# A higher priority for the split of the mixers' weights into high and low parts

## The chip, the cores and the metric

The kernel runs on one core of one Trainium2 chip. The metric is the device time in microseconds (us), the median over runs. Engines: PE is TensorE (matmuls; PEld its weight loads), DVE is VectorE, ACT is ScalarE, POOL is GpSimd, SP is SyncE, which here only issues DMAs.

## What is computed

Two layers of a network over 512 tokens of width 1024, all in float32. Each layer is a mixer followed by a mixture of experts, with norms, shifts, scales and gates (`mod`) that come from a small condition vector:

```python
for layer in range(DEPTH):                       # DEPTH = 2
    mod = cond @ w_ada[layer] + b_ada[layer]
    sh1, sc1, gt1, sh2, sc2, gt2 = jnp.split(mod[:, None, :], 6, axis=-1)
    u = rms_norm(h, norm1[layer]) * (1.0 + sc1) + sh1
    m = mixer_ab(u, ...) if layer % 2 == 0 else mixer_c(u, ...)
    h = h + gt1 * m
    u = rms_norm(h, norm2[layer]) * (1.0 + sc2) + sh2
    h = h + gt2 * hier_moe(u, ...)               # 32 experts, top 2 of one group
return rms_norm(h, final_norm)
```

Both mixers begin with a projection `u @ w_in` and end with one `y @ w_out`; between them, `mixer_ab` has a gated linear recurrence and a gated linear attention (4 heads), `mixer_c` a gated delta rule (8 heads, chunks, triangular solves).

## The kernel before

**Stages.** Layer 0's mixer runs from the start to about 295 us of the span, its router and experts to about 800 us; layer 1's mixer from 802 to about 1165 us, its router and experts to the end. The experts' stage goes through 16 pairs of experts, whose weights stream from HBM.

**The mixers' matmuls in three parts.** The mixers' matmuls take inputs of a rounded type (`F32R`). To keep float32 accuracy every factor is the sum of a high part, rounded, and a low part, the rest. `mm3` (L432) makes three matmuls of each pair: high by high (L435), high by low (L436), low by high (L437). For a weight block of 128 x 512, `split` (L424) makes the parts: ACT copies the raw block into `whi`, which rounds it (L428), and POOL subtracts `whi` from the raw block into `wlo` (L429). Both come from the pool `whl`, which has three buffers of each name. There are 136 such blocks. The input `u` gets its two parts in `u_block` (L552): ACT (L557), DVE (L558), and for the low part DVE or POOL by turns (L559).

**Steps.** A step is the work on one split block: `step_T` (L439) and `steps_rows` (L470) give pairs of functions, `prep`, which calls `split` (and, for output weights, first multiplies them by the gate, L480, on DVE and POOL by turns), and `mm`, a generator of the step's 12 matmuls. `run_steps` (L497) writes, ahead of step i, the `prep` of the steps up to i + 2; between the halves of a step it ticks the `Stream`, a small clock in which the other work of the mixers (gates, attention, keys, queries, solves, recurrences, modulation vectors) waits as generators with lags in ticks. Raw weight blocks are loaded by SP (L136) into a ring of two tiles; `raw_done` asks for the load of the next one when the last `split` that reads a tile has been written.

**What sets the order on an engine.** The program is written in one sequence, but the framework orders each engine's instructions anew: it plays the program through in a model of time, and at each point gives an engine, of those instructions whose inputs and buffers are there in the model, the one that ranks first. The rank is the place in the program. `tc.high_priority(PRI)` with `PRI = 80` ranks what is written inside it as if it stood 80 instructions earlier; before the change it is used for the first one-hot matrices of each layer's experts, for the gates' logits of `mixer_c` and for two exponentials of the router. `keep_in_program_order` ties an instruction behind the one written before it on its engine. On the chip each engine then runs its list strictly in that order, and waits at an instruction whose inputs or buffer are not there yet.

**Layer boundary.** At the end of layer 0 a loop over overflowing experts (`overflow`, L1718 to L1720; its count is read at run time) stands between the layers; all engines pass it together. Behind it `restart` (L1947) makes the row norms: ACT takes a square root (L419), DVE its reciprocal (L420), ACT and DVE scale a row block each (L1954, L1955), and PE turns the blocks (L564) before `u_block` makes `u`. `startup` (L1874) does the like in layer 0, with modulation vectors that it must compute first.

**Names that the prediction uses.** `yAhi`, `yAlo` (L673, L674): high and low parts of the linear recurrence's result, wanted by the first output steps. L755 `ex`: exponentials of the attention's decays; L792 `qs`: its scaled queries. In `mixer_c`: L1017 to L1020 the convolution and `Silu` of keys, queries and values (`kT`, `qT`, `vT`); L1035 the turning of the keys on PE; L1088 keys by queries; L1138 `X`, part of the triangular solve, and L1146 the matmuls that read it; L912 `orow`, the normed output rows, and L916 their turning.

Of the kernel before, what the change touches and what calls it, by code (L numbers as in the profile page):

```python
# [7 lines left out]
F32 = mybir.dt.float32  # L8
# [3 lines left out]
AF = mybir.ActivationFunctionType  # L12
# [16 lines left out]
PRI = 80  # L29
# [62 lines left out]
class Build:  # L92
# [331 lines left out]
    def split(self, src, shape):  # L424
        nc = self.nc
        hi = self.whl.tile(shape, F32R, name="whi", tag="whi")
        lo = self.whl.tile(shape, F32R, name="wlo", tag="wlo")
        nc.scalar.activation(hi, src, AF.Copy)  # L428
        nc.gpsimd.tensor_sub(lo, src, hi.bitcast(F32))  # L429
        return hi, lo  # L430

    def mm3(self, p, lhs, rhs, start, stop):  # L432
# [1563 lines left out]
```

## Time and profile before

| | |
|---|---|
| runs before | 1705.33, 1702.36, 1694.67 us; median 1702.36 |
| profiled execution | 1700.37 us; span 1698.2 us |
| mean granted clock of PE | 0.983 |
| busy: PE, DVE, ACT, POOL | 1623.4, 766.6, 522.6, 398.7 us |
| read from HBM | 492.21 MB, 291 GB/s over the span |

The span is the time between the first and the last event of the profiled execution; its own time, taken outside, is 2.2 us longer. A row of groups reads: line, engine, operation, output <- inputs, partitions x elements, count | busy us, mean ns of one | idle us of the engine just before them, with what ended that idle time. A row of waits reads: engine, what it was to make, line <- what it waited for: total us, times, longest. A row of the timeline reads: start us, duration us, engine, line, operation, count, and in brackets the idle time before it and what ended it. A row of windows reads: stretch, length, then busy us and count for PE, PEld, DVE, ACT and POOL, then PE's granted clock (1.00 is full), the DMA engines' mean busy share, and GB/s. SPq is the queue of SP.

### The profile page before, as it was taken

Reading aid. Unit: us, or ns where it says so; the run is one execution under the profiler, and the core shown is the slowest. Engines: PE = TensorE matmul, PEld = TensorE weight load, DVE = VectorE, ACT = ScalarE, POOL = GpSimd, SP = SyncE. Lnnn points to the kernel's source line nnn. Section 1 sums busy time; section 2 is a strip of 40 time slices with the busy share of each in tenths; the row PEclk is TensorE's granted clock in tenths of the full one; section 3 lists DMA queues with packets and bytes.
Section 4 is the critical chain, followed back from the end, with each engine's and each line's share of the span. In section 5 each row is a group of like instructions: output and inputs, shape, how many; then the busy total and the mean of one; then the engine's idle time right before and its main releaser. Section 6 shows DMA issues by size and latency. Waiting matters only on the chain. (4 is left out here: it accounts for less than half of the span.)

```text
span 1698.2 us, 23027 instructions
## 1 busy us (share of the span) xinstructions
PE 1623.4 (96%) x8890; PEld 973.7 (57%) x8890; DVE 766.6 (45%) x1770; ACT 522.6 (31%) x1034; POOL 398.7 (23%) x346
## 2 busy tenths in 40 slices
PE   6999999899999999998999999999899999999996
PEld 3665667454554555454666777787454555455453
DVE  2344553433333233234687787764324233233324
ACT  4665323210110111013646667555110111011013
POOL 2464542210100101001544353553100101001011
PEclk9999999999999999999899999999999999999998
DMA  8765646689999999995244333266699999999992
GB/s 306 230 216 172 247 162 227 264 350 386 414 411 413 413 411 414 411 411 158 75 154 146 125 103 122 75 224 233 231 374 412 412 411 414 411 412 413 412 406 99
DMA packets 156561, 496.02 MB, mean 292 GB/s; under 512 B 16472, under 2 KB 43668, under 8 KB 141088
## 3 DMA queue, kind: packets, MB, share of 16 engines
q1 hardware_dynamic: 155488, 493.23, 75.5%
q8 instruction: 72, 1.18, 0.3%
q10 hardware_dynamic: 960, 1.28, 0.2%
q14 instruction: 41, 0.34, 0.1%
HBM read 492.21 MB, written 2.10 MB: 291 GB/s over the span
## 5 line engine op out<-in xcount | busy, mean ns | idle before, releaser
L1538 PE MATMUL ps<-w,XTm 128*64 128x512 f32 x2048 | 447.1, 593 | 0.0
L1538 PEld LDWEIGHTS ps<-w,XTm 128*64 128x64 f32 x2048 | 161.7, 137 | 267.5 <-issue 260.2
L429 POOL TENSOR_TENSOR wlo<-w,whi 128x512 fp32r<-128x512 f32 x136 | 185.9, 1374 | 233.7 <-ACT whi L428 230.9
L1592 PE MATMUL ps<-w,hT 128*64 128x512 f32 (+1 forms) x1056 | 229.2, 584 | 1.0 <-ACT hT L1570 1.0
L1561 DVE TENSOR_TENSOR gg<-gg,ps 128x512 f32<-128x512 f32 x32 | 22.0, 687 | 377.8 <-PE ps L1538 377.7
L435 PE MATMUL ps<-w,whi 128*128 128x512 f32 x384 | 163.1, 425 | 0.4 <-ACT w L557 0.4
L436 PE MATMUL ps<-w,whi 128*128 128x512 f32 x384 | 154.1, 402 | 2.0 <-POOL w L559 1.5
L437 PE MATMUL ps<-w,wlo 128*128 128x512 f32 x384 | 153.7, 401 | 2.1 <-POOL wlo L429 2.1
L1592 PEld LDWEIGHTS ps<-w,hT 128*64 128x64 f32 x1056 | 81.8, 136 | 129.0 <-issue 116.0
L1615 DVE TENSOR_TENSOR w<-w,ps 128x512 f32<-128x512 f32 (+1 forms) x248 | 149.2, 662 | 6.9 <-PE ps L1606 5.5
L1547 POOL CAST sel<-ident 32x128 fp32r<-32x128 f32 x32 | 9.0, 280 | 590.4 <-PE ps L1575 532.7
L1596 POOL TENSOR_TENSOR yl<-y,yh 128x512 fp32r<-128x512 f32 x60 | 76.5, 1275 | 250.8 <-ACT yh L1595 250.8
L1595 ACT ACTIVATE yh<-y 128x512 fp32r<-128x512 f32 (+1 forms) x66 | 40.8, 618 | 294.5 <-DVE y L1594 293.6
L428 ACT ACTIVATE whi<-w 128x512 fp32r<-128x512 f32 x136 | 84.7, 627 | 143.9 <-PE ps L436 79.2
L1462 PE MATMUL ps<-Dm,hhi 128*128 128x256 f32 x512 | 125.8, 288 | 0.0
L1462 PE MATMUL ps<-Dm,hlo 128*128 128x256 f32 x512 | 123.3, 283 | 0.0
L1594 DVE SCALAR_TENSOR_TENSOR y<-ps,wsl,gate 128x512 f32<-128x512 f32 (+1 forms) x66 | 48.4, 734 | 150.5 <-issue 76.0
L1462 PEld LDWEIGHTS ps<-Dm,hhi 128*128 128x128 f32 x512 | 101.3, 198 | 13.5 <-issue 12.7
L1570 ACT ACTIVATE hT<-ps 128x512 f32<-128x512 f32 x32 | 19.1, 598 | 284.5 <-PE ps L1568 266.2
L1606 PE MATMUL ps<-yh,dt 128*128 128x512 f32 (+1 forms) x264 | 105.9, 406 | 0.0
L1462 PEld LDWEIGHTS ps<-Dm,hlo 128*128 128x128 f32 x512 | 101.3, 198 | 0.1
L1606 PE MATMUL ps<-yl,dt 128*128 128x512 f32 (+1 forms) x264 | 100.9, 387 | 0.0
(522 smaller groups left out, 2345.5 us busy)
## 6 DMA issues: line engine op xcount, KB each, us to landing
w<-in_moe_w_dram SPq DMA_DIRECT2D x380, 1024.0 KB
w<-in_w_ada_dram SPq DMA_DIRECT2D x40, 1024.0 KB
w<-in_w_in_c_dram SPq DMA_DIRECT2D x16, 1024.0 KB
w<-in_w_in_ab_dram SPq DMA_DIRECT2D x10, 1024.0 KB
wst<-in_w_ada_dram SPq DMA_DIRECT2D x8, 1024.0 KB
w<-in_w_out_ab_dram SPq DMA_DIRECT2D x4, 1024.0 KB
w<-in_moe_w_dram SPq DMA_DIRECT2D x8, 512.0 KB
w<-in_w_out_c_dram SPq DMA_DIRECT2D x4, 1024.0 KB
```

Of the source, the lines that this page charges most:

```text
L428: nc.scalar.activation(hi, src, AF.Copy)
L429: nc.gpsimd.tensor_sub(lo, src, hi.bitcast(F32))
L435: mm(p, lhs[0], rhs[0], start=start, stop=False)
L436: mm(p, lhs[0], rhs[1], start=False, stop=False)
L437: mm(p, lhs[1], rhs[0], start=False, stop=stop)
L1462: nc.tensor.matmul(p, spread(src[:, t], k // 4)[k % 4], Dm[:, t].rearrange("p e s -> p (e s)"), start=t + i == 0, stop=t == NT - 1 and i == 1)
L1538: self.nc.tensor.matmul(ps[j][half[e]], X[:, k, half[e]], w, start=k == 0, stop=k == KD - 1)
L1592: nc.tensor.matmul(py[half[e]], hT[:, k, half[e]], w, start=k == 0, stop=k == 3)
L1594: nc.vector.scalar_tensor_tensor(y32, py, wsl, gate[:, c], op0=OP.mult, op1=OP.mult)
L1596: (nc.vector if last else nc.gpsimd).tensor_sub(yl[:, c], y32, yh[:, c].bitcast(F32))
L1606: mm = nc.tensor.matmul(p, dt[:, t * P:(t + 1) * P], y[:, s], start=i == 0, stop=i == 1)
L1615: nc.vector.tensor_add(h, h, p)
```

## The change

The two instructions of `split` are written inside `tc.high_priority(PRI)`. Nothing else changes: the same instructions, tiles, buffers and loads.

```diff
@@ -425,8 +425,9 @@ def split(self, src, shape):
         hi = self.whl.tile(shape, F32R, name="whi", tag="whi")
         lo = self.whl.tile(shape, F32R, name="wlo", tag="wlo")
-        nc.scalar.activation(hi, src, AF.Copy)
-        nc.gpsimd.tensor_sub(lo, src, hi.bitcast(F32))
+        with self.tc.high_priority(PRI):
+            nc.scalar.activation(hi, src, AF.Copy)
+            nc.gpsimd.tensor_sub(lo, src, hi.bitcast(F32))
         return hi, lo
```

## The prediction

> **What bounds the kernel now.** I read the page first, then the busy time by stage, then what TensorE (PE) waited for in the two mixer stages, then the timeline at each such wait.
>
> ```profile
> span 1698.2 us, 23027 instructions
> PE 1623.4 (96%) x8890; PEld 973.7 (57%) x8890; DVE 766.6 (45%) x1770; ACT 522.6 (31%) x1034; POOL 398.7 (23%) x346
> ...
> L429 POOL TENSOR_TENSOR wlo<-w,whi 128x512 fp32r<-128x512 f32 x136 | 185.9, 1374 | 233.7 <-ACT whi L428 230.9
> ...
> L428 ACT ACTIVATE whi<-w 128x512 fp32r<-128x512 f32 x136 | 84.7, 627 | 143.9 <-PE ps L436 79.2
> ```
>
> PE is busy 96% of the span; nothing else is over 45%. The change touches two lines: 136 roundings `whi` on ScalarE (627 ns each) and 136 subtractions `wlo` on GpSimd (1374 ns each). GpSimd waits for `whi` before `wlo`, and `whi` waits for PE, which must give a buffer back.
>
> ```profile
> 802.00:1165.00 363.00, 344.20 (x2261) 261.98 (x2261) 265.59 (x773) 220.67 (x463) 167.58 (x144) 0.97 0.39 129
> 28.00:295.00 267.00, 257.02 (x1336) 175.46 (x1335) 123.10 (x231) 125.20 (x253) 121.14 (x84) 0.98 0.60 207
> ```
>
> ```profile
> 1320.00:1640.00 320.00, 320.00 (x1634) 168.40 (x1634) 103.27 (x191) 37.69 (x64) 28.31 (x30) 1.00 1.02 412
> ```
>
> The columns are the stretch, its length, the busy time of PE, PEld, DVE, ACT and POOL, PE's granted clock, the DMA share and GB/s. The splits lie in the first two stretches (mixer of layer 1, mixer of layer 0). There PE is idle 363.00 − 344.20 = 18.8 us and 267.00 − 257.02 = 10.0 us, and the clock below 1.00 costs another 0.03 × 363 = 10.9 and 0.02 × 267 = 5.3 us. All that the mixers can give is thus about 45 us, 2.6% of the time, whatever its cause. The expert stage (third row) has no idle PE time, so what a mixer gains or loses reaches the end nearly whole.
>
> **What PE waited for.** Of this idle time only a little is a split that came late:
>
> ```profile
> PE ps L437 <- POOL wlo L429: 2.1, 2, 1.7
> ...
> PE ps L436 <- POOL w L559: 1.5, 2, 1.2
> ...
> PE ps L436 <- POOL wlo L429: 1.0, 2, 0.7
> ```
>
> ```profile
> PE ps L916 <- ACT orow L912: 3.1, 3, 1.9
> PE ps L1035 <- ACT kT L1020: 2.6, 1, 2.6
> PE ps L1088 <- ACT qT L1020: 2.0, 2, 1.4
> ...
> PE ps L1146 <- ACT X L1138: 1.4, 1, 1.4
> ```
>
> The first list is layer 0 from 28 to 340 us, the second layer 1 from 800 to 1190 us (total us, times, longest). In layer 0 `wlo` holds PE up 2.1 + 1.0 = 3.1 us in four waits. In layer 1 no wait of PE over 0.4 us ends with a split; PE waits there for other ScalarE work, that of the delta-rule chains.
>
> **The change, part by part.** No instruction is added or removed, no size changed. Each `whi` and `wlo` is ranked as if written 80 instructions earlier. The ordering happens before the run, in the framework's own model of time: an engine takes, of what is ready there, what is ranked first. A rounding for step i+2 is written just ahead of step i and is ready when step i−1 has returned its buffer (three buffers). So it already stands ahead of all that step i calls up; what the 80 add is that it passes work of the few steps before: convolutions, gates, decays, and GpSimd's other multiplications. On ScalarE everything passed by one `whi` comes 0.63 us later, on GpSimd everything passed by one `wlo` comes 1.37 us later.
>
> *Gain 1: the late splits of layer 0.* These are the three waits of PE that can be found in the timeline, with what stood ahead:
>
> ```profile
> 118.48 0.50 PE L436 MATMUL ps<-wlo,w 128*128 128x512 f32 x1 [0.72 <-POOL wlo L429]
> 149.34 0.50 PE L437 MATMUL ps<-w,wlo 128*128 128x512 f32 x1 [0.43 <-POOL wlo L429]
> 158.41 0.51 PE L437 MATMUL ps<-w,wlo 128*128 128x512 f32 x1 [1.68 <-POOL wlo L429]
> ```
>
> ```profile
> 113.41 3.78 POOL L674 TENSOR_TENSOR yAlo<-xc,yAhi 128x512 fp32r<-128x512 f32 x3
> 117.14 3.77 POOL L429 TENSOR_TENSOR wlo<-w,whi 128x512 fp32r<-128x512 f32 x3
> ...
> 153.81 4.55 POOL L429 TENSOR_TENSOR wlo<-w,whi 128x512 fp32r<-128x512 f32 x1 [2.36 <-ACT whi L428]
> ```
>
> ```profile
> 152.09 0.63 ACT L755 ACTIVATE l<-l 128x512 f32<-128x512 f32 x1 [1.49 <-DVE l L765]
> 152.63 0.58 ACT L792 ACTIVATE qs<-ps 128x512 f32<-128x512 f32 x1
> 153.11 0.62 ACT L428 ACTIVATE whi<-w 128x512 fp32r<-128x512 f32 x1
> ```
>
> At 117.14 `wlo` stands behind three `yAlo` subtractions (3.78 us) that nobody needs before the output steps; passing them removes the 0.72 us. At 153.11 `whi` comes after a decay exponential and a copy, with 1.49 us of idle ScalarE just before; passing both brings it 1.2 us forward, and up to 2.7 us if it takes the idle slot, against 1.68 us wanted. I take the three waits whole: −0.72 − 0.43 − 1.68 = **−2.8 us**, bounds −2.8 and 0 (if in the model the split is not ready earlier). The 4.55 us `wlo` is not a matter of order: it takes 4.55 instead of the mean 1.37 us because it runs beside VectorE's decay work, and it will meet such work wherever it is put. By the Trainium skill ("SBUF — State Buffer", section on the two separate sides) VectorE and GpSimd share one port pair under an exclusive lock, so the later of two such instructions stands still until the first ends. By that rule the third wait would only shrink if `wlo` also started ahead of the VectorE instruction; without it the gain would be about −1.2 us instead of −2.8.
>
> *The start.* `whi` of step 2 is written after the first modulated blocks `u` (L557–L559) and is now ranked ahead of blocks 1 to 3.
>
> ```profile
> 28.73 2.98 POOL L429 TENSOR_TENSOR wlo<-w,whi 128x512 fp32r<-128x512 f32 x2 [26.66 <-ACT whi L428]
> 31.66 1.28 POOL L559 TENSOR_TENSOR w<-uf,w 128x512 fp32r<-128x512 f32 x1
> 32.90 1.74 POOL L429 TENSOR_TENSOR wlo<-w,whi 128x512 fp32r<-128x512 f32 x1
> 34.60 1.26 POOL L559 TENSOR_TENSOR w<-uf,w 128x512 fp32r<-128x512 f32 x1
> ```
>
> ```profile
> 35.92 0.50 PE L436 MATMUL ps<-w,whi 128*128 128x512 f32 x1 [1.24 <-POOL w L559]
> ```
>
> GpSimd's order becomes `wlo` three times, then `u` block 1, then block 3. Block 1 moves from 31.66 to about 28.73 + 2.98 + 1.37 = 33.1 and ends at 34.4; block 3 ends at about 35.6 instead of 35.86. PE waits longer for block 1 but is held by block 3 either way. Net −0.3 to +0.3 us; I take 0.
>
> *Cost 1: the layer boundary.* Behind the overflow loop of layer 0, ScalarE starts layer 1 with the row norms; PE stands still until the first normalised rows:
>
> ```profile
> 802.25 1.28 ACT L419 ACT_TABLE_LOAD   x1 [1.22 <-DVEq L1720]
> ...
> 804.11 1.93 ACT L1954 ACTIVATE hn<-w,hr 128x512 f32<-128x512 f32 x3
> ...
> 806.14 0.62 ACT L428 ACTIVATE whi<-w 128x512 fp32r<-128x512 f32 x1
> 806.66 0.71 ACT L1954 ACTIVATE hn<-w,hr 128x512 f32<-128x512 f32 x1
> 807.27 1.13 ACT L428 ACTIVATE whi<-w 128x512 fp32r<-128x512 f32 x2
> ```
>
> ```profile
> 804.87 3.87 PE L564 MATMUL ps<-ident,hn 128*128 128x128 f32 x16 [7.25 <-ACT hn L1954]
> ```
>
> Counting the code, some 55 instructions lie between the first norm and the first `whi`, fewer than 80, so two `whi` now go ahead of the norms: all of them come up to 2 × 0.57 = 1.1 us later. Part comes back, since these `whi` no longer stand around the last `hn` at 806.66. Bounds 0 and +1.1; I take **+0.6 us**.
>
> *Cost 2: the chains of layer 1.* Six waits of PE end there with ScalarE work that a `whi` can now pass (three `orow`, `kT`, two `qT`; `X` makes a seventh). Each grows by 0.63 us or not at all. With one in two, 7 × 0.5 × 0.63 = **+2.2 us**, bounds 0 and +4.4.
>
> *The loads.* A raw weight tile is free for its next load when its last `wlo` is done, so the change also moves transfers on SyncE's queue, where the loads of `w_ada` stand between those of the mixers' weights:
>
> ```profile
> SPq L136 <- POOL wlo L429: 269.5, 29, 18.9
> ```
>
> SyncE's queue waits 269.5 us for `wlo`. An earlier `wlo` starts the next raw load earlier by as much; nobody waits for that load now, and the DMA engines are at 0.39 and 0.60 in the two mixers. I cost it at 0. If a load of `w_ada` came late behind a raw one, PE would wait for it by the time that the split was moved, 1.4 us.
>
> The sum is −2.8 + 0 + 0.6 + 2.2 = **0.0 us**, within −3.1 and +5.8 by its own bounds. The profiled execution took 1700.37 us (span 1698.2); the median of the runs shown, 1702.36, lies 2.0 above it. I forecast the median: 1702.4 us. No change.
>
> **The rivals.**
>
> *A. The order hardly changes.* The three buffers, not the ranking, let a `whi` start, and it already stands ahead of its own step's work. For it: 38 of the waits of `whi` (79.2 us, L428 above) end with PE. Against it: the three `yAlo` at 113.41 are plainly in the way. Time 1702.4, the forecast's own.
>
> *B. Slower: the gap at the first key chain comes in every group.* The one long wait in layer 1 also cost clock:
>
> ```profile
> 838.28 1.12 PE L1035 MATMUL ps<-ident,kT 128*128 128x128 f32 x4 [2.62 <-ACT kT L1020]
> ```
>
> ```profile
> 835.00:840.00 5.00, 2.38 (x12) 1.40 (x9) 4.36 (x12) 4.62 (x7) 0.93 (x1) 0.80 0.55 160
> 840.00:845.00 5.00, 5.00 (x11) 3.27 (x11) 2.97 (x9) 4.96 (x13) 1.14 (x2) 0.50 0.15 50
> 845.00:850.00 5.00, 5.00 (x21) 4.07 (x20) 4.93 (x10) 2.26 (x5) 4.61 (x5) 0.68 0.00 0
> ```
>
> ScalarE is full there (4.62 and 4.96 of 5.00). PE lost 2.62 us, and at clocks of 0.80, 0.50 and 0.68 another 5 × (0.20 + 0.50 + 0.32) = 5.1 us: 7.7 us for one gap. A `whi` set early by the model, while PE on the chip has not yet returned its buffer, holds up the whole ScalarE queue with the key chain behind it. If that makes such a gap in the three other head groups too, the price is 3 × 7.7 = +23 us: **1725 us**. It decides from about two such gaps on (+15). Against it: in the other groups ScalarE has room, 220.67 of 363 us. By the Trainium skill ("TensorE: Matmul & The Clock Gate", Part 1) the clock falls only after an idle window of about 3.4 us and is then half. The trace agrees with the half (0.50), not quite with the length: 2.62 us in one wait were enough here. By the rule, gaps under 3.4 us would cost only themselves, and B would be three times 2.6, +8 us.
>
> *C. Faster: the splits feed PE through its gaps.* With weights split earlier the model finds main matmuls to put where PE now waits. Then the `kT` gap goes with its clock (−7.7), the three waits (−2.8), the waits for L559 at the start (−1.5): −12.0, **1690 us**. Against it: PE was given L1035 at 838.28 because the model thought `kT` ready, not for lack of matmuls. A stronger form, half of the mixers' 45 us, gives 1680.
>
> **How the numbers follow.** About 1%, 17 us, is what can be told from no change here. Chances: forecast 0.52 (1699 to 1708 by its bounds), A 0.22, B 0.13, C 0.09, its stronger form 0.04. B alone is slower by over 1%, with a little from the forecast's edge: 0.14. Faster by over 1% needs the stronger form, or C and luck: 0.06. The rest, 0.80. For eight in ten I take the bounds of the sum, the runs' own spread (1694.67 to 1705.33), C on the low side and one or two more clock gaps on the high side: 1690 to 1714.
>
> **What would show it.** Right: `wlo` at 117 ahead of `yAlo`; PE's waits for `wlo` in layer 0 gone; the wait at 804.87 up to 1.1 us longer; PE's wait for `kT` and `qT` in layer 1 within 4 us of now; idle PE in both mixers together within 6 us of 28.8. Wrong: more windows with a clock near 0.50 between 850 and 1160 us (B), or the clock at 1.00 from 835 to 850 (C).

## The result, and the profile after

The changed kernel takes 1717.41 us (median of 4 runs, 1714.99 to 1727.67), the kernel before 1702.86 us beside it (4 runs, 1694.67 to 1705.33). The ratio is 1.0116, with a 95% interval from 1.0092 to 1.0140: slower by about 1%, where the forecast was no change, 1702.4 us, within 1690 to 1714. One execution of the kernel before took 4140 us, against 1695 to 1708 us in all the others, and is left out of the means and ratios below. The profiled execution of the changed kernel took 1714.99 us, its span is 1713.1. Its lines carry numbers one higher than before from L429 on.

The page of the changed kernel, first the engines, then the two moved instructions:

```profile
span 1713.1 us, 23034 instructions
PE 1629.6 (95%) x8890; PEld 976.4 (57%) x8890; DVE 774.0 (45%) x1770; ACT 527.2 (31%) x1036; POOL 392.9 (23%) x346
...
L430 POOL TENSOR_TENSOR wlo<-w,whi 128x512 fp32r<-128x512 f32 x136 | 179.4, 1322 | 282.1 <-ACT whi L429 270.4
...
L429 ACT ACTIVATE whi<-w 128x512 fp32r<-128x512 f32 x136 | 84.7, 627 | 140.5 <-PE ps L437 84.8
```

The splits themselves cost no more than before (1322 and 627 ns each). ScalarE has two instructions more, 1036 for 1034. Both are loads of a table for an activation function; one of them is shown below. PE's busy time grew by 6.2 us although it does the same 8890 matmuls: part of them ran at a lower clock. The three stretches of the prediction, with ends moved by what the changed kernel is late there (a row of windows gives the stretch, its length, the busy time of PE, PEld, DVE, ACT and POOL, then the clock):

```profile
28.00:296.00 268.00, 257.80 (x1337) 176.65 (x1336) 124.85 (x232) 126.81 (x253) 116.17 (x84) 0.97 0.61 206
803.00:1180.00 377.00, 350.62 (x2262) 263.73 (x2262) 271.00 (x773) 224.45 (x466) 166.86 (x144) 0.96 0.37 122
1334.00:1654.00 320.00, 320.00 (x1638) 168.52 (x1638) 102.41 (x190) 38.15 (x64) 28.55 (x31) 1.00 1.02 412
```

In 320 us of the expert stage PE does as many matmuls as before (1638, before 1634) at the full clock, so nothing is won or lost there. Layer 0's mixer is 1 us longer; layer 1's mixer takes 377 us for the matmuls that took 363, with idle PE time of 26.4 instead of 18.8 us and a clock of 0.96 instead of 0.97. So nearly all of the loss is in layer 1's mixer. What PE waited for there (from 797 to 845 us, then from 840 to 1240 us):

```profile
PE ps L565 <- DMA br<-in_moe_b_rt_dram: 9.7, 1, 9.7
```

```profile
PE ps L1211 <- DVE vn L1205: 4.4, 3, 2.4
PE ps L1147 <- ACT X L1139: 3.7, 1, 3.7
```

Three waits are longer or new, none of them for a split. The wait for the first normalised rows was 7.25 us (the releaser named, a small load, had landed long before; what PE needs is `hn`). The wait of 3.7 us for `X` was 1.4 us. The wait of 2.4 us for `vn` is new: at these first `vn` copies the kernel before had none (its longest wait for `vn`, 1.4 us, comes at 1084 us, and the changed kernel has it too). In the changed kernel the clock falls behind both:

```profile
995.90:999.30 3.40, 1.25 (x7) 0.77 (x7) 3.37 (x6) 0.39 (x2) 2.21 (x2) 1.00 0.01 2
999.30:1006.10 6.80, 6.58 (x16) 3.79 (x16) 4.85 (x9) 4.37 (x10) 1.27 (x1) 0.50 0.00 1
1050.50:1053.90 3.40, 0.97 (x4) 0.27 (x4) 3.16 (x12) 3.35 (x7) 1.72 (x2) 1.00 0.53 186
1053.90:1067.60 13.70, 13.65 (x131) 9.46 (x131) 4.67 (x17) 6.55 (x15) 1.90 (x2) 0.50 0.24 78
```

In the first and third rows PE is busy 1.25 and 0.97 of 3.40 us; in the rows that follow it is busy all the time, at a granted clock of 0.50. These 6.8 + 13.7 us at half speed lose 10.2 us. The kernel before has no such stretch between 860 and 1158 us. Ahead of its first use of `vn`, at 994.91 us, and behind its wait for `X`, which ends at 1042.91 us, its rows are:

```profile
988.00:995.00 7.00, 7.00 (x47) 5.92 (x44) 6.47 (x19) 6.02 (x10) 5.39 (x5) 1.00 0.07 26
1043.00:1060.00 17.00, 16.85 (x196) 12.41 (x196) 10.47 (x28) 13.87 (x28) 6.67 (x7) 1.00 0.39 124
```

In return the profiled execution of the changed kernel has no fall at the `kT` gap, where the kernel before had one of 10.2 us. How much clock an execution loses varies: over the changed kernel's four executions the span times the clock is 1674 to 1679 us, and the rest of the span, what the lower clock cost, is 34 to 52 us.

**What delays the three waits.** At the boundary, ScalarE of the changed kernel:

```profile
803.37 1.28 ACT L429 ACT_TABLE_LOAD   x1 [1.23 <-DVEq L1721]
804.66 1.15 ACT L429 ACTIVATE whi<-w 128x512 fp32r<-128x512 f32 x2
805.83 1.28 ACT L419 ACT_TABLE_LOAD   x1
807.12 0.67 ACT L419 ACTIVATE hr<-hsq 128x1 f32<-128x1 f32 x3
```

As forecast, two roundings go ahead of the norms (1.15 us). Not forecast: they bring a table load of their own. The first activation behind the branch at L1721 loads a table, here one for the Copy of `whi`, and the square root of the norms then needs another: 1.28 us twice instead of once. The norms start 2.45 us later against the loop's end, and PE waits 9.7 us for them instead of 7.25, then once more for 0.9 us.

At the first `vn` copies, GpSimd and VectorE of the changed kernel:

```profile
990.40 1.29 POOL L430 TENSOR_TENSOR wlo<-w,whi 128x512 fp32r<-128x512 f32 x1 [0.74 <-ACT whi L429]
```

```profile
990.51 1.20 DVE L413 TENSOR_TENSOR rsz<-rsz,rsx 128x4 f32<-128x4 f32 x1
```

The same instruction in the kernel before:

```profile
987.81 0.16 DVE L413 TENSOR_TENSOR rsz<-rsz,rsx 128x4 f32<-128x4 f32 x1
```

The small instructions of the inverse square root (128x4, L412 to L414) take 0.16 us each; the one that meets `wlo` takes 1.20. Before, GpSimd was idle while this series ran (987.62 to 989.6 us); two `wlo` came in a row at 994.56. From L410 to L1054 in this key chain VectorE now meets `wlo` and the `sq` and `qg` multiplications behind it, and the `vn` copies at its end come some 4.6 us later in the span (999.19 for 994.58). VectorE had been 2.35 us late when the series began (L409 at 987.77 for 985.42); the rest, 2.3 us, came about in it and behind it. PE, too, was late, but less (1.7 us at the matmuls of L1089), and so has to wait.

At the `X` copies, ScalarE of the kernel before, then of the changed one:

```profile
1032.92 0.20 ACT L905 ACTIVATE or<-or 128x2 f32<-128x2 f32 x1
1033.03 0.58 ACT L350 ACTIVATE modrow<-ps 128x512 f32<-128x512 f32 x1
...
1042.21 2.69 ACT L1138 ACTIVATE X<-Yt 32x256 f32<-32x256 f32 x4
```

```profile
1040.92 0.20 ACT L906 ACTIVATE or<-or 128x2 f32<-128x2 f32 x1
1041.36 0.63 ACT L429 ACTIVATE whi<-w 128x512 fp32r<-128x512 f32 x1 [0.24 <-PE ps L437]
1041.90 0.61 ACT L913 ACTIVATE orow<-ps,or 128x128 f32<-128x128 f32 x2
1042.40 0.60 ACT L350 ACTIVATE modrow<-ps 128x512 f32<-128x512 f32 x1
1042.88 0.70 ACT L1018 ACTIVATE kT<-ps,cv 128x512 f32<-128x512 f32 x1
1043.03 2.15 ACTq L357 DMA_DIRECT2D modst<-modrow  x4
1045.43 0.63 ACT L429 ACTIVATE whi<-w 128x512 fp32r<-128x512 f32 x1 [1.86 <-PE ps L437]
...
1052.23 2.69 ACT L1139 ACTIVATE X<-Yt 32x256 f32<-32x256 f32 x4
```

ACTq is ScalarE's own queue, in which its DMA issues take their turn. Before, `modrow` came directly behind the square root `or`, its four DMA issues followed, and the `orow` copies ran between them. Now a rounding that still waits for PE (0.24), and the two `orow`, stand ahead of `modrow`; the issues, 2.15 us of this queue, start later by that much, and a second rounding stands behind them, ahead of the squares. From `or` to the first `X` copy it was 9.3 us (1032.92 to 1042.21); now it is 11.3 us (1040.92 to 1052.23).

### The profile page after: what moved, and what is told of

Read it like the earlier page. It is cut to its first block, busy times and chain, and to the rows that moved or that the text cites. A ratio compares the mean times of both kernels' runs of the same rounds, so it can differ in the third digit from the quotient of the medians.

```text
span 1713.1 us, 23034 instructions
## 1 busy us (share of the span) xinstructions
PE 1629.6 (95%) x8890; PEld 976.4 (57%) x8890; DVE 774.0 (45%) x1770; ACT 527.2 (31%) x1036; POOL 392.9 (23%) x346
## 3 DMA queue, kind: packets, MB, share of 16 engines
q10 hardware_dynamic: 960, 1.28, 0.2%
## 5 line engine op out<-in xcount | busy, mean ns | idle before, releaser
L430 POOL TENSOR_TENSOR wlo<-w,whi 128x512 fp32r<-128x512 f32 x136 | 179.4, 1322 | 282.1 <-ACT whi L429 270.4
L429 ACT ACTIVATE whi<-w 128x512 fp32r<-128x512 f32 x136 | 84.7, 627 | 140.5 <-PE ps L437 84.8
```

## The experiments

Sixteen kernels were run, each beside the kernel before on the same chip (on four chips in all). Two things can be read from every execution: its span, and the mean clock granted. Span × (1 − clock) is what the clock cost; "rest" is the span without it. The last two columns are the means over a kernel's executions, less those of the kernel before on the same chip (1670 to 1671 us of rest, 26 to 28 us of clock). A mean has an uncertainty of about 1 us (2 to 3 where a kernel has only four executions).

| kernel | splits moved up | median us | before us | ratio (95%) | rest, us | clock, us |
|---|---|---|---|---|---|---|
| e_l0 | 56, layer 0 | 1701.99 | 1698.33 | 1.0020 (1.0006 to 1.0034) | −1.9 | +5.1 |
| e_l1 | 80, layer 1 | 1714.74 | 1698.33 | 1.0085 (1.0059 to 1.0111) | +7.6 | +8.5 |
| e_ev1 | all but 3 | 1712.39 | 1698.33 | 1.0092 (1.0058 to 1.0126) | +4.1 | +11.0 |
| e_ev2 | all but 4 | 1712.71 | 1698.33 | 1.0095 (1.0073 to 1.0117) | +3.9 | +11.4 |
| e_bnd1 | 3 | 1702.34 | 1699.48 | 1.0022 (1.0011 to 1.0033) | +1.9 | +1.8 |
| e_bnd0 | all but 3 | 1711.86 | 1699.48 | 1.0083 (1.0063 to 1.0103) | +5.5 | +7.8 |
| e_mid1 | 23 | 1708.68 | 1699.48 | 1.0067 (1.0046 to 1.0088) | +4.7 | +6.9 |
| e_on2c | 2 | 1706.05 | 1699.54 | 1.0045 (1.0030 to 1.0060) | +2.7 | +3.6 |
| e_hi | 110 | 1700.92 | 1699.54 | 1.0003 (0.9992 to 1.0014) | −0.3 | +1.1 |
| e_l0b12 | 44, layer 0 | 1699.47 | 1699.54 | 1.0001 (0.9990 to 1.0013) | −0.9 | +0.5 |
| e_midw8 | 23, 8 dummies | 1706.09 | 1700.13 | 1.0037 (1.0020 to 1.0055) | +2.8 | +3.5 |
| e_on2w8 | 2, 8 dummies | 1705.79 | 1700.13 | 1.0036 (1.0022 to 1.0050) | +1.7 | +4.2 |
| e_bw8 | none, 8 dummies | 1700.16 | 1700.13 | 1.0002 (0.9989 to 1.0015) | +0.8 | −0.6 |
| e_wk9 | none, 9 dummies | 1701.48 | 1700.13 | 1.0004 (0.9991 to 1.0016) | +3.4 | −1.7 |
| e_co80 | none, chains up | 1702.74 | 1699.54 | 1.0026 (1.0012 to 1.0040) | +0.4 | +3.9 |
| e_ch80 | 136, chains up | 1755.4 | 1699.48 | 1.0343 (1.0319 to 1.0367) | +55.3 | +2.4 |

The theory at the start: the moved splits delay layer 1's chains, and two waits of PE (2.4 and 3.7 us) become long enough to bring the clock down. One fact stands in the planned programs and needs no run: with the priority on the line of `wlo` alone, the planned order of every engine is that of the kernel before; with it on `whi` alone, it is the changed kernel's but for two places on GpSimd. What moves everything is `whi` on ScalarE.

**One layer at a time (e_l0, e_l1).** The priority becomes a value that mixer_c sets when it begins.

```
-        with self.tc.high_priority(PRI):
+        with self.tc.high_priority(self.rank):     # PRI and 0, or 0 and PRI
...
-        self.solved, self.gates_known = 0, False
+        self.solved, self.gates_known, self.rank = 0, False, 0
```

> Priority in layer 0's mixer only; in layer 1's the splits keep the place where they are written. Theory (two waits of PE in layer 1's chains, of 2.4 and 3.7 us, that let the clock fall): the places disappear, layer 0 ends 1.1 us later as in the changed kernel, so 1704 us (1699 to 1708), within 0.3% of before; clock near 0.50 in layer 1's mixer only where before has it (about 838, 1159 and 1193 us). Rival (accident: any other order moves the falls of the clock about, by ten us either way): the falls in layer 1 lie elsewhere although its order is that of before, and the time is off by 5 us or more.

> Priority in layer 1's mixer only. Theory: the whole loss is here, so 1716 us (1712 to 1720), ratio 1.007 to 1.011, with the waits at the vn copies (L1211, 2.4 us) and at the X copies (L1147, 3.7 us) as in the changed kernel and the clock near 0.50 behind both. Rival (the loss needs layer 0's order as well, by what it leaves behind, or it was an accident of that one program): under 1708 us.

1.0020 and 1.0085: the theory's numbers. In e_l1's profile both waits are there (2.3 and 3.7 us) with 17.1 us of half clock behind the second. In e_l0's, layer 1 has the waits of before. What was not expected is e_l0's way to +0.2%: its rest is shorter by 1.9 us, its clock costs 5.1 us more. Its profile, from one of its fastest executions, shows only a part of that: a stretch of 3.4 us at half clock at 34 us, behind a wait for `u` at the start that is 1.8 us now and was 1.2.

**Two places undone in the changed kernel (e_ev1, e_ev2).** Splits are counted by `n` from 0.

```
+        with self.tc.high_priority(0 if 96 <= self.n <= 98 else PRI):     # e_ev1
+        with self.tc.high_priority(0 if 106 <= self.n <= 109 else PRI):   # e_ev2
```

> The changed kernel, but three splits (the 97th to the 99th, those just ahead of the wait of 2.4 us at the vn copies) keep their written place. Theory: this wait and the clock's fall behind it are gone, -5.9 us; if the second place stays, 1711 us (1708 to 1714); the orders of ScalarE and VectorE also change in the second place here, so that it may go too (down to 1704). Rival (these two roundings are not the cause: the chain is late anyway): 1717, the fall of the clock still between 995 and 1010 us.

> The changed kernel, but four splits (the 107th to the 110th, those around the wait of 3.7 us at the X copies) keep their written place; PE's order is the same as in the changed kernel. Theory: in ScalarE's queue two roundings no longer stand ahead of the X copies, the wait sinks to about 1.4 us, the clock stays up, -8.1 us: 1709 us (1706 to 1713). The first place stays as it is (-0). Rival (the copies are late because VectorE or the DMA issues on ScalarE's queue are late, the roundings cost only their own 1.3 us): 1716, and the clock still falls near 1055 us.

Both missed: 1.0092 and 1.0095, with the waits still there (2.1 us at L1211 in e_ev1, 3.5 us at L1147 in e_ev2). They are no proof for the rival either, since putting three or four splits back let the planner place other work anew. In e_ev2 ScalarE between the squares and the `X` copies:

```profile
1047.41 1.28 ACT L1060 ACT_TABLE_LOAD   x1
1048.71 0.63 ACT L1060 ACTIVATE E<-E 128x512 f32<-128x512 f32 x1
1049.35 1.28 ACT L1021 ACT_TABLE_LOAD   x1
1050.65 0.63 ACT L1021 ACTIVATE kT<-kT 128x512 f32<-128x512 f32 x1
1051.28 1.28 ACT L1063 ACT_TABLE_LOAD   x1
```

The exponential of `E` now stands ahead of the Silu of `kT`, and between exponential, Silu and exponential three tables are loaded where two were. 1.28 us of table replaced the roundings, and the `X` copies were as late as ever. So the question was put the other way round: start from the kernel before and move a few.

**A few splits moved in the kernel before (e_bnd1, e_mid1, e_on2c), and the complements (e_bnd0, e_hi).**

```
+        with self.tc.high_priority(PRI if 56 <= self.n <= 58 else 0):     # e_bnd1
+        with self.tc.high_priority(0 if 56 <= self.n <= 58 else PRI):     # e_bnd0
+        with self.tc.high_priority(PRI if 90 <= self.n <= 112 else 0):    # e_mid1
+        with self.tc.high_priority(PRI if 106 <= self.n <= 107 else 0):   # e_on2c
```

e_hi has PRI for all `n` but 56 to 58 and 90 to 112.

> The kernel before, with only the first three splits of layer 1 moved up; on PE and VectorE the order is that of before, on ScalarE two roundings and a table load of their own now stand ahead of the norms. Theory (boundary): rounding 2 x 0.55 and one more table load of 1.28 us ahead of the norms, and VectorE's first norm beside GpSimd's wlo (1.55 instead of 0.49 us): PE waits 9.7 instead of 7.2 us at L565 and starts layer 1 some 3 us later; with one more stretch of half clock +3 to +5 us, ratio 1.0015 to 1.003. Rival (layer 1 takes it back, as the changed kernel did at 846 to 854 us, -4): 1.000 within 0.001.

> The changed kernel, with only the first three splits of layer 1 at their written place (the mirror of the run before). Theory: the wait at L565 is 7.2 us again, 3 to 5 us less than the changed kernel: against the kernel before 1.008 to 1.010, where the changed kernel had 1.0116. Rival (no part of the loss lies here): 1.011 to 1.013.

> The kernel before, with only the splits 91 to 113 moved up, those around the two waits at the vn and X copies. Theory (the splits that pass the chains there are what makes the chains late): the waits of 2.1 to 2.4 and of 3.5 to 4.3 us appear, PE's idle time in this stretch is 7.5 instead of 3.8 us, the clock falls behind them (7 to 20 us at half speed, which loses 3 to 10 us): +7 to +14 us, ratio 1.004 to 1.008. Rival (the chains come there already late from the splits before, 57 to 90, and have slack without them): the waits stay at 1.4 us, ratio under 1.002.

> The kernel before, with two splits only (the 107th and 108th) moved up. PE's order is that of before; on ScalarE one rounding now stands ahead of the modulation row and one among the squares, and as a knock-on the exponential of E comes ahead of the Silu of kT, which takes one more table load. Theory (ScalarE's queue ahead of the X copies is all that matters here): rounding 0.55 and a table load of 1.28 us and the kT convolution behind the DMA issues make the X copies some 2 us later, PE's wait at L1147 3.3 to 3.9 instead of 1.4 us, and the clock falls behind it (3 to 14 us at half speed): +3.5 to +8 us, ratio 1.002 to 1.005. Rival (two splits alone do not do it, the chain must come late already): wait under 2 us, ratio within 0.001 of 1.

> The changed kernel without its two costly places: the first three splits of layer 1 and the 91st to the 113th stay where they are written, the other 110 are moved up. Theory (the loss sits in these places): layer 0's share alone is left, ratio 1.000 to 1.003, L565 waits 7.2 us, no wait over 2.7 us between 850 and 1240. Rival (every moved split costs a little): in proportion to 110 of 136, 1.009.

All five came as the theory said (e_hi but for a wait of 3.1 us at L1671, in the router, which the kernel before has too). Three splits at the boundary cost 0.22%; the order of PE and of VectorE is that of before, and ScalarE shows why:

```profile
801.07 1.28 ACT L429 ACT_TABLE_LOAD   x1 [1.21 <-DVEq L1721]
802.36 1.15 ACT L429 ACTIVATE whi<-w 128x512 fp32r<-128x512 f32 x2
803.53 1.28 ACT L419 ACT_TABLE_LOAD   x1
```

Putting them back in the changed kernel leaves 1.0083 of 1.0116. The 23 splits in the middle cost 0.67%; the longest waits of e_mid1 from 970 to 1070 us are those of the changed kernel, to a tenth (the 2.9 us for `vn` are two waits, of 2.4 and 0.5 us; the kernel before has none there):

```profile
PE ps L1147 <- ACT X L1139: 3.7, 1, 3.7
PE ps L1211 <- DVE vn L1205: 2.9, 2, 2.4
```

Two splits alone (e_on2c), with PE's order untouched, cost 0.45%, and the wait at L1147 is 4.3 us. The other 110 of 136 (e_hi) cost nothing that can be measured, 1.0003: there is no wait at the first `vn` copies, and that for `X` is 1.4 us again. Boundary and middle add up to 0.22 + 0.67 = 0.89%, which is what all of layer 1's splits cost (e_l1, 0.85%), against 1.16% for the whole. Layer 0 alone had 0.20%, but e_hi, which moves its 56 splits too, only 0.03%. So the 0.27% that remain have no sure place; the intervals of these figures are about as wide.

**Layer 0 without its start (e_l0b12).** `PRI if 12 <= self.n <= 55 else 0`.

> The kernel before, with only the 13th to the 56th split moved up: layer 0's mixer without its start. Theory (the forecast's first gain was real, and the start is what layer 0 lost): the waits for wlo near 118, 149 and 158 us go, -2 to -3 us, ratio 0.998 to 0.999. Rival (the gain is eaten inside layer 0, as its waits move to other work or to the clock): 1.000 to 1.002.

1.0001: the rival. Its profile from 28 to 341 us says how:

```profile
PE ps L436 <- ACT whi L429: 1.2, 1, 1.2
...
PE ps L437 <- POOL wlo L430: 0.9, 1, 0.9
```

The 3.1 us of waits for `wlo` are now 0.9 us, but a wait for `whi` of 1.2 us is new: PE's idle time in the layer falls only by 1.6 us (worked out from the trace's matmuls), and the mean over the executions gives −0.9 in the rest and +0.5 in the clock.

**Dummy matmuls in the wait (e_midw8, e_on2w8, e_bw8, e_wk9).** These ask how much of the price is the clock.

```
-            lo32 = slice(0, 32)
+            lo32 = self.warm(8 if g.i == 2 else 0) or slice(0, 32)
```

`warm(n)` writes n matmuls of constants and returns nothing. Eight of them go into PE's queue six matmuls ahead of L1147; no other instruction of any engine changes place in e_midw8 and e_bw8 (in e_on2w8 a handful do, none of PE's). e_wk9 has nine ahead of the first transposes of `kT`.

> As the run with the splits 91 to 113 moved up (1.0067), with eight dummy matmuls of no use (bf16, 128x512, 0.23 us each) in PE's queue shortly ahead of the X copies' wait of 3.7 us; every other instruction stays in its place. PE then reaches the wait 1.9 us later. Theory (the clock's fall behind this wait is most of the price): PE idles 1.8 instead of 3.7 us there, the clock stays up, and though more work is done the time falls by 4 to 6 us: ratio 1.003 to 1.0045. Rival (the wait itself is the price): 1.0067, unchanged within 0.001.

> As the run with two splits moved up (1.0045), with the same eight dummy matmuls. Theory: the wait of 4.3 us becomes 2.4 us; this is near the bound from which the clock falls (idle 1.9 of 3.4 us in the traces so far), so part of the loss goes: ratio 1.002 to 1.0035. Rival: 1.0045 unchanged.

> Control: the kernel before with the same eight dummy matmuls. The wait there is 1.4 us and has no fall of the clock behind it, so the dummies outlast it by 0.4 us: ratio 1.000 (0.999 to 1.0015) by every theory; a gain here would mean that the dummies help in some other way.

> The kernel before with nine dummy matmuls (2.1 us) ahead of the first kT transposes, the wait of 2.6 us behind which its clock is at half speed for 10.2 us; a few instructions of ScalarE and VectorE near it change places. Theory (the fall is avoidable): up to -5 us, ratio 0.997 to 0.999. Rival (the dummies only take the place of the wait, or the shifted order brings another one): 1.000 or more.

e_midw8 does more work than e_mid1 and is faster, 1.0037 against 1.0067 (the intervals overlap slightly; the profiles differ plainly). First e_mid1, then e_midw8, around the wait:

```profile
1046.80:1050.20 3.40, 0.00 (x0) 0.00 (x0) 2.85 (x14) 3.37 (x7) 0.94 (x1) 1.00 0.78 266
1050.20:1063.90 13.70, 13.63 (x119) 8.37 (x123) 4.61 (x13) 7.58 (x17) 2.69 (x4) 0.50 0.24 77
```

```profile
1043.10:1046.50 3.40, 2.20 (x10) 1.32 (x8) 2.18 (x14) 3.37 (x9) 0.27 (x1) 1.00 0.95 290
1046.50:1049.90 3.40, 2.50 (x40) 0.99 (x40) 2.52 (x5) 3.31 (x6) 1.45 (x2) 1.00 0.02 5
```

In e_mid1 PE is idle for a whole 3.40 us and then runs 13.7 us at 0.50. With the dummies (8 in 1.89 us) the wait is 1.95 us and lies in two such stretches, 1.2 us in one and 0.8 in the other; the clock stays at 1.00. Not all that e_midw8 gains need come from this wait. In its profile the clock does not fall behind `vn` either, although that wait is 2.37 us as before: it, too, happens to lie across two stretches (0.75 and 1.61 us). So the profile shows what a wait split in two does; that the dummies help rests on the twelve executions, whose mean clock cost is 3.5 us above the kernel before, where e_mid1's is 6.9. The control gains nothing (1.0002). In e_on2w8 the wait is still 2.5 us, PE idles 2.5 us of one stretch, and the fall is still there: 1.0036 against 1.0045, not told apart. e_wk9 missed: the fall at `kT` shrank from 10.2 to 3.4 us, but a wait for `qT` of 3.6 us took its place a little later.

**The chains moved up (e_co80, e_ch80).** In the kernel before, 80 for the convolutions, squares, the exponential of `E`, the `X` and `vn` copies (e_co80); in the changed kernel, 80 for everything that the chains issue (e_ch80).

> The kernel before (splits as written), with the chains' work on ScalarE and VectorE in layer 1 moved up by 80 instead: convolutions with Silu, squares, the exponential of E, the X and vn copies. Theory (what counts is how early the chains stand, not how early the splits do): two table loads fewer, the waits of 1.4 to 2.6 us at kT, qT, X and vn shrink, ratio 0.994 to 0.999. Rival (the splits now come late in their turn and PE waits for wlo): 1.002 or more.

> The changed kernel, with all work of layer 1's chains (convolutions, keys, queries, values, solve, recurrence, outputs; not the modulation vectors) ranked 80 up as well, so that the splits pass them no more than before. Theory (the splits hurt only by passing the chains): no wait of PE on a chain over 2 us between 850 and 1240, the clock near 0.50 there for at most 7 us, ratio 0.992 to 1.002. Rival (it is the changed order as such; another one brings other waits): waits on other work, gates or modulation, over 2 us, and 1.005 or more.

Both missed. e_co80 has two table loads fewer in the plan, but a wait of 2.9 and one of 3.9 us in the chains. e_ch80 has little idle time in layer 1 but for one wait of 4.0 us, and little half clock, nearly as the theory wanted, and is 56 us slower for a reason that no theory named. PE's matmuls for the modulation vectors, e_ch80 first, then the changed kernel, from 850 us to the mixer's end:

```profile
L260 PE MATMUL ps<-w,cond 128*32 128x512 f32 x126 | 63.7, 612 | 0.0
```

```profile
L260 PE MATMUL ps<-w,cond 128*32 128x512 f32 x128 | 22.0, 633 | 0.0
```

One takes as long as ever (612 and 633 ns), but four that follow each other run side by side, each on 32 of PE's columns; scattered among the others, each takes PE alone. This line alone is busy 41.7 us more; where the other 14 us of the loss lie was not traced.

## Why the prediction was wrong, point by point

- **What can be gained or lost.** The expert stage passed the loss on whole, as forecast. The 45 us that the mixers can give bound a gain only: e_ch80 lost 56.
- **Gain 1 (−2.8).** Half right. `wlo` does go ahead of `yAlo` (113.40, three `yAlo` at 115.10), and the waits for `wlo` fall from 3.1 to 0.9 us. But a wait for `whi` of 1.2 us appears, and without the start (e_l0b12) −0.9 us of rest and +0.5 of clock is all that comes of it: no gain that can be measured, where −2.8 us had been taken.
- **The start (0).** The order came as forecast, and the wait for block 1 or 3 is 1.9 instead of 1.2 us at its longest. What was left out is again the clock: of the seven kernels that move the first splits, five show a stretch of 3.4 us at 0.50 that begins at 34 to 37 us and loses 1.7 us; none of the eleven others does. The clock costs 5.1 us with these splits (e_l0) and 0.5 without (e_l0b12), but e_hi, with them, has only 1.1, so their price is not settled.
- **Cost 1 (+0.6, bounds 0 and +1.1).** Mis-sized, beyond its bounds: e_bnd1 measures 0.22%, 3.7 us. Seen rightly were the two roundings (1.15 us); missing were the second table load (1.28 us) and one more stretch of half clock, 13.7 instead of 10.2 us in e_bnd1's profile (its mean clock cost is +1.8 us).
- **Cost 2 (+2.2, bounds 0 and +4.4).** The step that failed. It took seven waits that were there already, all ended by ScalarE, and let each grow by one rounding (0.63 us) or not at all, by itself. e_mid1 measures 0.67%, 11.4 us, from two waits. One is for `vn`, which VectorE makes: it was not among the seven, did not exist at this place, and is 2.4 us long. The other is that for `X`, which grew by 2.3 us and not by 0.63. Together these 4.7 us lie just above the bounds that were given. The larger part by the table's means (6.9 us), the clock that falls behind both, was left out of the sum. Left out, too, were the ways by which the delay came about: at `X` the DMA issues on ScalarE's queue with a rounding ahead of them, at `vn` `wlo` meeting VectorE's small instructions.
- **The loads (0).** Nothing in the trace speaks against it: PE's waits for `w_ada` are 1.2 us in all, before 1.5.
- **Rival B** was the one that came, in its kind: waits in the chains that bring the clock down, decided by two of them. It had been given 0.13 and a place, the `kT` gap, where none came; it was priced at 7.7 us a gap, 15 for two, and two cost 11.4. By the Trainium skill ("TensorE: Matmul & The Clock Gate", Part 1) idle gaps under about 3.4 us should have cost themselves alone. The trace differs: the first fall came behind a wait of 2.4 us; the second wait, 3.7 us, is longer than that. Of e_mid1's loss 6.9 us on the mean are clock and 4.7 the rest. With one wait filled with work of no use the loss is some 5 us smaller, with the reservation made above.
- **Rival A** is refuted: the order changes on every engine. **Rival C** did not come: the clock fall at `kT` was gone in the profiled execution of the changed kernel, but it is there again in e_ev1 and e_ev2, whose wait there is the same 2.2 us, so that was chance (in the changed kernel this wait lies across two windows of the clock's grid; see the last section).

What stays open: why the planner's own model put `whi` there. And of the two waits, e_on2c shows the part of the second by itself; the first was not run alone. How much of the loss is clock in itself rests on the mean clock of few executions and on one comparison, e_mid1 with e_midw8, whose intervals overlap.

## What to carry to other kernels

A priority does not only bring its own instructions forward: on engines that work in order, each one delays all behind it, so look for what stands at the few places where the main engine waits, and price those, not an average over all places; here 26 of 136 moved splits cost 0.89 of the 1.16%, and the 110 others alone nothing that can be measured. When a wait of PE is priced, look whether the clock falls behind it: that can cost more than the wait. When a change of order is to be taken apart, move a few instructions in the kernel before and keep PE's order; undoing a few in the changed kernel brings in new differences.

## What was not expected of the hardware

- **The clock is decided on a fixed grid.** In each of the 18 profiles all changes of the clock lie whole multiples of 3.413 us apart. Cutting the profiles (from 40 to 1670 us) into these windows: after a window at full clock in which PE was idle 2.0 us or more, the next window was at half clock in 84 of 84 cases; with 1.75 to 2.0 us in 20 of 24; with 1.5 to 1.75 us in 5 of 21; below that in 45 of some 8200. The same wait of about 2.35 us for `vn` brought the clock down where it lay in one window (2.37 us in e_ev2, 2.35 in e_mid1), and did not where it lay across two (1.08 and 1.25 us in e_l1, 0.75 and 1.61 in e_midw8). Where the grid lies differs from profile to profile, which is probably one reason why executions of one kernel differ by 10 us. It is a reason, too, not to take the falls of one profile for the kernel's.
- **Idle time is not all that counts.** 16 of those 45 cases have no idle time at all. In the kernel before, PE is busy without a break from 189.43 to 192.84 us, with small matmuls (64x64, 64x32), and runs at 0.50 from 192.84 to 196.25 us. What lowers the clock there stays open.
- **A small VectorE instruction that meets GpSimd's 128x512 subtraction takes 1.20 instead of 0.16 us.** The rows of L413 above show it.
- **Copy has a table too, when it comes first behind a branch.** At L429 it took a load of 1.28 us of its own, in the changed kernel and in e_bnd1.
- **In these two programs matmuls of 32 columns shared PE only when they followed each other**: 22.0 us for 128 of them together, 63.7 us for 126 scattered.
